# Feed-forward blocks taken in pairs with one accumulation per pair, and a norm without ordering edges, in a two-layer RWKV-7 / S5 trunk

## The chip, the cores and the metric

The kernel runs on one core of a Trainium2 chip. The metric is the device time of one execution in microseconds; a run's time is compared as the median of several. Engines are named as in the profile: PE (TensorE, matmul), PEld (TensorE's weight loads), DVE (VectorE), ACT (ScalarE), POOL (GpSimd), SP (SyncE, which issues most DMAs).

## What is computed

Two layers over 1024 frames of 1024 channels, in float32. Layer 0 mixes in time by an RWKV-7 recurrence, layer 1 by an S5 diagonal state-space layer with GELU and a gated output. After each mixer comes a feed-forward block, and every sub-layer ends in a norm:

```python
def sq_relu_mlp(x, w1, w2):
    return jnp.square(jax.nn.relu(x @ w1)) @ w2          # w1 1024x4096, w2 4096x1024

def reference(x, ...):
    h = x
    for i in range(2):
        mix = rwkv7_time_mix(h, ...) if i == 0 else s5_mix(h, ...)
        h = layer_norm(ALPHA * h + mix, ln_g[2 * i], ln_b[2 * i])
        h = layer_norm(ALPHA * h + sq_relu_mlp(h, mlp_w1[i], mlp_w2[i]), ln_g[2 * i + 1], ln_b[2 * i + 1])
    return h
```

## The kernel before

**Layout and precision.** Activations lie with channels on the 128 partitions and frames along the free dimension. The 1024 frames are two halves, A (`hA`, H = 0) and B (`hB`, H = 1), of 512 frames; a half is eight tiles of 128x512. A float32 product is made of three matmuls (`mm3`, line 258): each operand is split into a high part (a ScalarE cast, line 191) and a low part (a VectorE subtraction, line 192), and high x high, high x low and low x high are added up in one PSUM bank. Weights come by DMA as 128x512 pieces (`wraw`), are split into `whi` and `wlo` (three buffers each, `wraw` two), and each piece serves twelve matmuls. For the first three blocks of layer 1 the low parts of the weights are made beforehand (`presplit`) and loaded, so those blocks need only the cast (line 224).

**Feed-forward in blocks** (`blocks`, line 1110 on). The 4096 hidden channels are 16 blocks of 256. `up(b)` computes two 128x512 tiles of hidden channels, 24 matmuls into one bank each; ScalarE empties the bank with Relu (line 1126), squares (line 1127), and the result is split into `qbuf` (four slots, two for even and two for odd blocks). `down(b)` multiplies by the second weight matrix: four column groups `n2` of two tiles; each of the eight output tiles takes 6 matmuls in a bank of its own, and VectorE adds the bank to `h` (line 1158; line 1156 for the first block, which also scales by ALPHA). Banks come in rotation from `psd()`: three in layer 0 (`narrow`), seven in layer 1's feed-forward (`wide`).

`mlp` runs a half in layer 0 with the up phase one block ahead:

```python
up(0)
for b in range(nb):
    if b + 1 < nb: up(b + 1)
    down(b, b == 0)
    yield
```

**Order of the work.** A list scheduler orders each engine's instructions at compile time: lower priority numbers first, in a simulated time. `rank(base)` sets the number for what is traced inside it, and the feed-forward of layer 0 runs from 200000. So the rest of the recurrence, output projection, norms (99000) and S5 (99300, 99400) go ahead of it and its matmuls fill the gaps; the S5 tables (300000) come behind it. Work of another stage is also spread by hand: `first_steps` makes a generator's steps ready, and `weave` advances them behind each split (share `PACEU`) and each addition (share `PACED`); `behind` then adds an ordering edge, so that the woven VectorE instruction comes after the one that it is woven behind. `INS1`, `INS3` and `PREB` count the calls of `mlp` after which half B's output projection is traced, S5's result is loaded and the presplit starts.

**Layer 1's feed-forward.** Blocks 0 to 2 (`JB` = 3) of half A run alone (`ua`, `da`) while half B gets its norm (`second_half`, woven). Then `both` takes blocks 3 to 15 of the two halves together with sums and differences of operands (`tops`: T1 to T4, made of `hA` and `hB`; T1 goes into the buffer of `qbuf`, `t1b`). Then blocks 0 to 2 of half B run alone (`ub`, `db`), the last two of them by column halves of 256 frames with kept weights (`keep`, `kept`), so that `last_norm` of the first 256 frames can run beside the second.

Of the kernel before, what the change touches and what calls it, by code (L numbers as in the profile page):

```python
# [18 lines left out]
HT = 512  # L19
KT = 8  # L20
L = 64
KB2 = 2
INS1 = 12
INS2 = 13
VSH = (-1, 2, 2, 4, 64)
INS3 = 12
PACE = None
LN1R = -1
WO0R = 99000
# [3 lines left out]
TB = 2  # L33
LN2R = 99000
PAUSE = 8
PRE = 6
PACEU = (2.0, 7.0)
PACED = (0.5, 1.3)
PREB = 3
JB = 3  # L40
TABB = 6
LN8R = 400000
# [37 lines left out]
def trunk(ctx, tc, A):  # L80
# [102 lines left out]
    def unweave():  # L183
        while woven:
            steps, base = woven.pop(0)
            with rank(base):
                for _ in steps:
                    pass
# [15 lines left out]
    nw = [0]  # L204

    low = {}

    def wload(src, kt, n, key=None, halved=False):

        step = 512 // n  # L210
        out = []
        for k0 in range(0, kt, step):
            kept = low.get((key, k0)) if key else None
            raw = wp.tile([128, step, n], F32, tag="wraw", name="wraw", bufs=2)
            SP.dma_start(raw, src[:, k0 : k0 + step])
            hi = wp.tile([128, step, n], F32R, tag="whi", name="whi")
            lo = wp.tile([128, step, n], F32R, tag="wlo", name="wlo")
            nw[0] += 1
            if halved:
                S.mul(hi, raw, 0.5)  # L220
                weave(V.scalar_tensor_tensor(lo, raw, 0.5, hi.bitcast(F32), op0=ALU.mult, op1=ALU.subtract))
            elif kept is not None:
                SP.dma_start(lo.bitcast(F32).rearrange("p k n -> p (k n)"), kept)
                S.copy(hi, raw)
            else:
                split(raw, hi, lo, G if nw[0] % WLG[0] in WLG[1] and WLG[2] <= nw[0] < WLG[3] else V)
                if key and key[0] not in ("mw1", "mw2"):
                    low[key, k0] = dr.tile([128, 512], F32, name=f"low{len(low)}")
                    SP.dma_start(low[key, k0], lo.bitcast(F32).rearrange("p k n -> p (k n)"))
            out += [(hi[:, k], lo[:, k]) for k in range(step)]  # L230
        return out
# [26 lines left out]
    def mm3(p, whi, wlo, xh, xl, first, last):  # L258
        mmb(p, whi, xh, start=first, stop=False)
        mmb(p, whi, xl, start=False, stop=False)  # L260
        mmb(p, wlo, xh, start=False, stop=last)
# [18 lines left out]
    def dense(p, w, xs):  # L280
        n = len(xs)
        for k in range(n):
            mm3(p, w[k][0], w[k][1], xs[k][0], xs[k][1], k == 0, k == n - 1)
# [15 lines left out]
    def psd():  # L299
        pool, tag = banks[0][nb[0] % len(banks[0])]  # L300
        nb[0] += 1
        return pool.tile([128, HT], F32, tag=tag, name="d")
# [811 lines left out]
    def blocks(i, h, xo, qbuf):  # L1114

        nw = 512 // KB2
        qs = {}

        def up(b):
            qs[b] = []  # L1120
            pace_[0] = PACEU[i]
            for n in range(KB2):
                p = psd()
                dense(p, wload(A["mw1"][i, b * KB2 + n], KT, 128, ("mw1", i, b * KB2 + n)), xo)
                r = tp.tile([128, HT], F32, tag="ev", name="rl", bufs=EVB)
                S.activation(r, p, AF.Relu)  # L1126
                S.activation(r, r, AF.Square)
                qt = qbuf[:, n + KB2 * (b % 2)]
                split(r, qt[:, 0], qt[:, 1])
                qs[b].append((qt[:, 0], qt[:, 1]))  # L1130
            pace_[0] = 1.0

        def kept(src, part):
            raw = wp.tile([128, KB2, nw], F32, tag="wraw", name="wraw", bufs=2)
            SP.dma_start(raw, src)
            hi, lo = (jp.tile([128, HT], F32R, tag=t, name="k" + t, bufs=8).rearrange("p (k n) -> p k n", k=KB2)
                      for t in ("t1", "t2"))
            SP.dma_start(lo.bitcast(F32).rearrange("p k n -> p (k n)"), part)
            S.copy(hi, raw)
            return [(hi[:, k], lo[:, k]) for k in range(KB2)]  # L1140

        def down(b, first=False, cs=slice(0, HT), keep=None):
            for n2 in range(C // nw):
                if keep is None:
                    w = wload(A["mw2"][i, b, n2], KB2, nw, ("mw2", i, b, n2))
                else:
                    if (b, n2) not in keep:
                        keep[b, n2] = kept(A["mw2"][i, b, n2], low[("mw2", i, b, n2), 0])
                    w = keep[b, n2]
                for n in range(nw // 128):  # L1150
                    p = psd()[:, cs]
                    dense(p, [(x[:, n * 128 : (n + 1) * 128], y[:, n * 128 : (n + 1) * 128]) for x, y in w],
                          [(x[:, cs], y[:, cs]) for x, y in qs[b]])
                    z = h[n2 * (nw // 128) + n][:, cs]
                    if first:
                        weave(V.scalar_tensor_tensor(z, z, ALPHA, p, op0=ALU.mult, op1=ALU.add), PACED[i])
                    else:
                        weave(V.tensor_add(z, z, p), PACED[i])  # L1158

        return up, down  # L1160

    def mlp(i, h, xo, qbuf):

        nb = 32 // KB2
        up, down = blocks(i, h, xo, qbuf)
        up(0)
        for b in range(nb):
            if b + 1 < nb:
                up(b + 1)
            down(b, b == 0)  # L1170
            yield

    def both(i, hP, hQ, P, Q, tops, first):
# [400 lines left out]
    def first_steps(steps, base):  # L1574
        with rank(base):
            next(steps)
            woven.append([steps, tc.cur_priority])
# [66 lines left out]
    def second_half():  # L1644
        yield from norm_steps(hB, 2, 1, True, xoB)
        for k in range(4):
            a = t3[k]
            G.tensor_add(a, a, hB[k])
            d = [jp.tile([128, HT], F32R, tag="t2", name="t2", bufs=8) for _ in range(2)]
            split(a, *d)  # L1650
            yield 1
            tops[1].append(d)

    ua, da = blocks(1, hA, xo, qbuf)
    ua(0)
    first_steps(second_half(), 99000)
    for b in range(JB - 1):
        ua(b + 1)
        da(b, b == 0)
    unweave()  # L1660
    t1b = qtile()
    with rank(99100):
        for k in range(4):
# [5 lines left out]
        for k in range(4):  # L1669
            V.tensor_sub(t3[k], t3[k], hB[k + 4])  # L1670
            tops[3].append(operand(t3[k]))
    da(JB - 1, JB == 1)
    uj, dj = both(1, hB, hA, xoB, xo, tops, JB)
    uj(JB)
    for b in range(JB + 1, NB):
# [6 lines left out]
    with rank(99000):  # L1682
        layer_norm(hA, 3, 0, False)
    store(0, hA)
    for b in range(JB - TB):
        ub(b + 1)
        db(b)
    for b in range(JB - TB + 1, JB):
        ub(b)
    keep = {}  # L1690
    for c in range(2):
        for b in range(JB - TB, JB):
            db(b, False, slice(256 * c, 256 * c + 256), keep)
        if c == 0:
            with rank(LN8R):
                early = last_norm(hB, 3, 0)
                next(early)
# [74 lines left out]
```

## Time and profile before

| | |
|---|---|
| median of 3 runs | 2596.31 us (2596.01 to 2599.6) |
| the profiled execution | 2585.47 us, its span 2583.5 us |
| PE busy | 2466.0 us (95%), 16684 matmuls |
| DVE busy | 1794.0 us (69%) |
| ACT busy | 1210.5 us (47%) |
| POOL busy | 406.0 us (16%) |
| granted TensorE clock, mean | 0.975 |
| moved by DMA | 340.66 MB |

Shares are of the span. A matmul's recorded time overlaps its neighbours', so a busy PE is not a PE at its peak. Rows of the waits view read "engine line waited for: us in total, times, longest". Rows of the timeline give start, length, engine, line, operation, output<-inputs, shape, count, and in brackets the idle time before with what ended it.

### The profile page before, as it was taken

What the parts mean: (1) busy time and instruction counts of PE and PEld (TensorE: products, weight loads), DVE (VectorE), ACT (ScalarE), POOL (GpSimd) and SP (SyncE); (2) the same over time, 40 slices, a digit from 0 to 9 for tenths busy, and PEclk for the clock granted to TensorE, in tenths of its full rate; (3) what the DMA queues carried; (4) which work ended last, traced back from release to release, by engine and by line L of the source; (5) the groups of instructions that cost most, each with busy time, mean ns of one, the idle gap of its engine ahead of it and who ended that gap; (6) DMA issues with size and microseconds to landing.
All of it is one profiled execution on the core that took longest, in us unless ns stands there. A gap on an engine that the chain in (4) does not pass through costs nothing.

```text
span 2583.5 us, 43873 instructions
## 1 busy us (share of the span) xinstructions
PE 2466.0 (95%) x16684; PEld 2002.0 (77%) x16684; DVE 1794.0 (69%) x3443; ACT 1210.5 (47%) x2165; POOL 406.0 (16%) x336
## 2 busy tenths in 40 slices
PE   7989989989989999999999999999999999999997
PEld 5779767788767888777777878887887888888886
DVE  7477687577787776899886665676657555656555
ACT  7555575454454443345634444334565333343334
POOL 3110441331211102001000000100222111111111
PEclk9999989999899999999999999999999999999998
DMA  4765455664222324446565553244261111111233
GB/s 152 261 200 184 160 198 172 190 186 152 93 70 78 104 86 126 141 122 165 162 226 192 176 175 111 95 162 160 94 197 60 49 54 50 48 58 49 78 122 114
DMA packets 217682, 340.66 MB, mean 132 GB/s; under 512 B 21248, under 2 KB 81792, under 8 KB 217472
## 3 DMA queue, kind: packets, MB, share of 16 engines
q1 hardware_dynamic: 216320, 335.77, 40.9%
q8 instruction: 131, 2.15, 0.4%
q10 hardware_dynamic: 1152, 2.10, 0.2%
q14 instruction: 79, 0.65, 0.1%
HBM read 267.53 MB, written 70.25 MB: 131 GB/s over the span
## 4 chain that ended last, share of the span: by engine, by line
PE 69%; DVE 13%; DMA 9%; ACT 5%; issue 3%; SPq 1%; POOL 0%; ACTq 0%; DVEq 0%; POOLq 0%
PE d L256 51%; PE d L1195 10%; DVE wlo L192 2%; PE pA L672 1%; DMA wraw<-in_mw_dram 1%; ACT whi L191 1%; DMA yl<-s_y 1%; DVE hA L1158 1%; DMA pre<-in_mw_dram 1%; DMA ldsg<-s_sg 1%; DMA s_y<-yg 1%; PE pR L780 1%; DMA lda<-s_a 1%; DVE oAl L192 1%; PE pq L934 1%
## 5 line engine op out<-in xcount | busy, mean ns | idle before, releaser
L191 ACT CAST whi<-wraw 128x512 fp32r<-128x512 f32 x424 | 261.6, 619 | 487.1 <-PE d L256 249.8
L192 DVE TENSOR_TENSOR wlo<-wraw,whi 128x512 fp32r<-128x512 f32 x424 | 317.4, 750 | 201.1 <-ACT whi L191 197.2
L256 PE MATMUL d<-qbuf,whi 128*128 128x512 f32 x1152 | 365.2, 399 | 9.8 <-ACT rl L1126 4.7
L256 PE MATMUL d<-oAh,whi 128*128 128x512 f32 (+1 forms) x752 | 303.2, 409 | 13.1 <-ACT ev L493 5.5
L256 PE MATMUL d<-oAl,whi 128*128 128x512 f32 (+1 forms) x752 | 302.1, 403 | 7.7 <-DVE oAl L942 4.4
L256 PE MATMUL d<-oAh,wlo 128*128 128x512 f32 (+1 forms) x752 | 301.2, 404 | 3.5 <-DMA wlo<-low 1.9
L256 PEld LDWEIGHTS d<-qbuf,whi 128*128 128x128 f32 x1152 | 212.2, 189 | 63.1 <-DVE hA L1158 7.8
L256 PE MATMUL d<-qbuf,wlo 128*128 128x512 f32 x576 | 225.5, 394 | 0.0
L256 PE MATMUL d<-oBh,whi 128*128 128x512 f32 x496 | 195.9, 395 | 0.4 <-DVE hA L1158 0.4
L256 PE MATMUL d<-oBh,wlo 128*128 128x512 f32 x496 | 195.8, 395 | 0.0
L256 PE MATMUL d<-oBl,whi 128*128 128x512 f32 x496 | 193.7, 391 | 0.0
L256 PEld LDWEIGHTS d<-oAh,whi 128*128 128x128 f32 (+1 forms) x752 | 143.1, 192 | 48.0 <-ACT ev L493 7.8
L256 PEld LDWEIGHTS d<-oAl,whi 128*128 128x128 f32 (+1 forms) x752 | 144.4, 193 | 38.7 <-DVE oAl L942 4.8
L256 PEld LDWEIGHTS d<-oAh,wlo 128*128 128x128 f32 (+1 forms) x752 | 144.3, 193 | 36.2 <-DVE wlo L192 2.7
L256 PE MATMUL d<-ql,whi 128*128 128x512 f32 x416 | 163.1, 392 | 0.0
L256 PE MATMUL d<-qh,whi 128*128 128x512 f32 x416 | 162.0, 389 | 0.0
L256 PE MATMUL d<-qh,wlo 128*128 128x512 f32 x416 | 158.0, 394 | 0.0
L256 PEld LDWEIGHTS d<-qbuf,wlo 128*128 128x128 f32 x576 | 108.9, 189 | 24.4 <-issue 0.5
L1158 DVE TENSOR_TENSOR hA<-hA,d 128x512 f32<-128x512 f32 x136 | 92.0, 683 | 28.8 <-PE d L256 27.7
L1158 DVE TENSOR_TENSOR hB<-hB,d 128x512 f32<-128x512 f32 (+1 forms) x160 | 97.6, 631 | 20.1 <-PE d L256 18.9
L256 PEld LDWEIGHTS d<-oBh,wlo 128*128 128x128 f32 x496 | 93.2, 188 | 21.9 <-issue 0.8
L256 PEld LDWEIGHTS d<-oBh,whi 128*128 128x128 f32 x496 | 93.3, 188 | 21.5 <-issue 2.0
(495 smaller groups left out, 5268.6 us busy)
## 6 DMA issues: line engine op xcount, KB each, us to landing
wraw<-in_mw_dram SPq DMA_DIRECT2D x356, 256.0 KB, 2.7
wlo<-low SPq DMA_DIRECT2D x92, 256.0 KB, 2.9
wraw<-in_glu_dram SPq DMA_DIRECT2D x64, 256.0 KB, 2.7
low<-wlo SPq DMA_DIRECT2D x52, 256.0 KB, 2.6
raw<-in_mw_dram SPq DMA_DIRECT2D x52, 256.0 KB, 2.7
wraw<-in_wk_dram SPq DMA_DIRECT2D x32, 256.0 KB, 3.2
wraw<-in_wr_dram SPq DMA_DIRECT2D x32, 256.0 KB, 3.7
wraw<-in_wv_dram SPq DMA_DIRECT2D x32, 256.0 KB, 4.2
```

Source lines behind the costliest of these rows:

```text
L191: S.copy(hi, src)
L192: op = (e or V).tensor_sub(lo, src, hi.bitcast(F32))
L256: bulk.append((PE.matmul(p, w, x, **kw).ins, x.shape[-1]))
L672: prods.append(PE.matmul(pp[h][:, cc, i], D.KB[j][hs, u].rearrange("p j l -> p (j l)"), D.AR[j][hs, u].rearrange("p j l -> p (j l)"), star ...
L780: hop.append(PE.matmul(pR[hs, i], at[:, h, c, i, 0], vsa[:, cl, h, i], start=True, stop=True))
L934: PE.matmul(pq[:, j : j + 1], q[:, j * 128 : (j + 1) * 128], ones_c[:, 0:1], start=k + j == 0, stop=k == KT - 1, skip_group_check=True)
L1158: weave(V.tensor_add(z, z, p), PACED[i])
L1195: PE.matmul(p, w[:, k], x, start=not add and k + j == 0, stop=k == 3 and j == 2, skip_group_check=True)
```

## The change

`down` takes a tuple of blocks and adds up all their products for an output tile in one bank, so that VectorE adds to `h` once per tuple. `mlp` and layer 1's blocks alone call it with pairs. The up phases of both blocks of a pair stand ahead of its down phase. The products of a column group are ordered by block; in the first group (`n2 == 0`) of a pair the second block's two operands are taken one after the other over both output tiles. In layer 1 half B's norm and T2 are traced at once under rank 99000, without weaving and so without ordering edges, behind the first up phase; blocks 0 and 1 of half A form a pair and block 2 stands alone. At the end, the last two blocks form a pair within each column half. `INS1` and `INS3` go from 12 calls to 6, `PREB` from 3 to 1, and the shares `PACEU` and `PACED` of layer 1 change, where nothing is woven in `blocks` any more.

```diff
-INS1 = 12
+INS1 = 6
-INS3 = 12
+INS3 = 6
-PACEU = (2.0, 7.0)
-PACED = (0.5, 1.3)
-PREB = 3
+PACEU = (2.0, 6.0)
+PACED = (0.5, 2.0)
+PREB = 1
...
-        def down(b, first=False, cs=slice(0, HT), keep=None):
+        def down(bs, first=False, cs=slice(0, HT), keep=None):
             for n2 in range(C // nw):
...
+                ws = []
+                for b in bs:
+                    if keep is None:
+                        ws.append(wload(A["mw2"][i, b, n2], KB2, nw, ("mw2", i, b, n2)))
...
+                nn = nw // 128
+                ps = [psd()[:, cs] for _ in range(nn)]
+                parts = [(w[k], qs[b][k]) for w, b in zip(ws, bs) for k in range(KB2)]
...
+                last = len(parts) - 1
+                groups = [range(KB2 * m, KB2 * m + KB2) for m in range(len(bs))]
+                if n2 == 0 and len(bs) > 1:
+                    groups[-1:] = [(j,) for j in groups[-1]]
+                turns_ = [(n, js) for js in groups for n in range(nn)]
+                for n, js in turns_:
+                    products(n, js)
+                    if last not in js:
+                        continue
+                    z, p = h[n2 * nn + n][:, cs], ps[n]
...
     def mlp(i, h, xo, qbuf):
...
-        up(0)
-        for b in range(nb):
-            if b + 1 < nb:
-                up(b + 1)
-            down(b, b == 0)
+        for b in range(0, 32 // KB2, 2):
+            up(b)
+            up(b + 1)
+            down((b, b + 1), b == 0)
             yield
...
     ua(0)
-    first_steps(second_half(), 99000)
-    for b in range(JB - 1):
-        ua(b + 1)
-        da(b, b == 0)
-    unweave()
+    with rank(99000):
+        run(second_half())
+    ua(1)
+    da((0, 1), True)
+    ua(2)
...
-    da(JB - 1, JB == 1)
+    da((2,))
...
-    for b in range(JB - TB):
-        ub(b + 1)
-        db(b)
-    for b in range(JB - TB + 1, JB):
-        ub(b)
+    ub(1)
+    db((0,))
+    ub(2)
     keep = {}
     for c in range(2):
-        for b in range(JB - TB, JB):
-            db(b, False, slice(256 * c, 256 * c + 256), keep)
+        db(tuple(range(JB - TB, JB)), False, slice(256 * c, 256 * c + 256), keep)
```

More of the change, by code (lines that the diff above doesn't have):

```diff
@@ L1140, in kept, with products @@
             return [(hi[:, k], lo[:, k]) for k in range(KB2)]
-        def down(b, first=False, cs=slice(0, HT), keep=None):
+        def down(bs, first=False, cs=slice(0, HT), keep=None):
             for n2 in range(C // nw):
[L1144 to L1154, printed above, removed]
+                ws = []
+                for b in bs:
+                    if keep is None:
+                        ws.append(wload(A["mw2"][i, b, n2], KB2, nw, ("mw2", i, b, n2)))
+                    else:
+                        if (b, n2) not in keep:
+                            keep[b, n2] = kept(A["mw2"][i, b, n2], low[("mw2", i, b, n2), 0])
+                        ws.append(keep[b, n2])
+                nn = nw // 128
+                ps = [psd()[:, cs] for _ in range(nn)]
+                parts = [(w[k], qs[b][k]) for w, b in zip(ws, bs) for k in range(KB2)]
+                def products(n, js):
+                    for j in js:
+                        (x, y), (qh, ql) = parts[j]
+                        sl = slice(n * 128, (n + 1) * 128)
+                        mm3(ps[n], x[:, sl], y[:, sl], qh[:, cs], ql[:, cs], j == 0, j == len(parts) - 1)
+                last = len(parts) - 1
[8 more added lines that the diff above has]
+                    z, p = h[n2 * nn + n][:, cs], ps[n]
                     if first:
@@ L1162, in mlp @@
     def mlp(i, h, xo, qbuf):
-        nb = 32 // KB2
         up, down = blocks(i, h, xo, qbuf)
-        up(0)
-        for b in range(nb):
-            if b + 1 < nb:
-                up(b + 1)
-            down(b, b == 0)
+        for b in range(0, 32 // KB2, 2):
+            up(b)
+            up(b + 1)
+            down((b, b + 1), b == 0)
             yield
```

## The prediction

> **What bounds the kernel now.** I read the page's busy times first, then the stages as stretches, then TensorE's waits stage by stage, then the timeline at the places where the edit acts.
>
> ```profile
> PE 2466.0 (95%) x16684; PEld 2002.0 (77%) x16684; DVE 1794.0 (69%) x3443; ACT 1210.5 (47%) x2165; POOL 406.0 (16%) x336
> L1158 DVE TENSOR_TENSOR hA<-hA,d 128x512 f32<-128x512 f32 x136 | 92.0, 683 | 28.8 <-PE d L256 27.7
> L1158 DVE TENSOR_TENSOR hB<-hB,d 128x512 f32<-128x512 f32 (+1 forms) x160 | 97.6, 631 | 20.1 <-PE d L256 18.9
> ```
>
> TensorE is busy 95% of the span; the edit changes neither the number of matmuls (16684) nor their shapes. It can only fill or open gaps in TensorE's stream. The stages (columns: length, then busy time of PE, PEld, DVE, ACT, POOL, then the granted clock and DMA):
>
> ```profile
> 740.00:1020.00 280.00, 275.03 (x2170) 220.09 (x2169) 210.29 (x459) 123.90 (x226) 38.57 (x30) 0.99 0.31 93
> 1020.00:1280.00 260.00, 252.50 (x1288) 196.02 (x1287) 233.75 (x452) 125.01 (x228) 23.02 (x18) 0.99 0.52 149
> 1280.00:1570.00 290.00, 281.27 (x2011) 227.89 (x2009) 194.75 (x359) 129.23 (x227) 0.00 (x0) 1.00 0.56 188
> ```
>
> From 740 to 1640 runs layer 0's feed-forward for both halves, mixed with the end of the recurrence, the S5 tables and S5. TensorE idles there 5.0, 7.5 and 8.7 us in the three rows: this is all that the pairs can win. What ended TensorE's idle times from 740 to 1570, and then from 1885 to the end (us in total, times, longest):
>
> ```profile
> PE d L256 <- ACT rl L1126: 4.7, 6, 1.6
> PE d L256 <- DVE hA L1158: 3.9, 5, 1.8
> ...
> PE d L256 <- DVE hA L1156: 0.7, 1, 0.7
> ```
>
> ```profile
> PE d L1195 <- DVE wlo L192: 4.1, 1, 4.1
> PE d L256 <- ACT rl L1126: 2.2, 1, 2.2
> ...
> PE d L256 <- DVE hA L1158: 0.6, 1, 0.6
> ```
>
> The waits on L1156 and L1158 are for a PSUM bank that the addition into h has not yet emptied; those on L1126 for a bank that the Relu has not yet emptied. The rest of the idle time in the first stretch belongs to the recurrence, the S5 tables and S5, out of the edit's reach.
>
> **The change part by part.**
>
> *One addition per pair.* Full-width additions fall from 136 to 64 on hA and from 128 to 64 on hB, and the 32 half-width ones of the last stage to 16. At 0.683 us each that is 136 x 0.683 = 93 us less VectorE work (16 half ones at some 0.4 us make it about 100), so VectorE goes from 1794 to about 1695. By itself this shortens nothing, VectorE not being the bound. What counts is the bank waits. Matmuls come every 0.2287 us:
>
> ```profile
> 1559.65 93.09 PE d L256 x407
> ```
>
> Before, a bank of the down phase took 6 matmuls, 1.37 us, and with three banks in rotation was wanted back 2 x 1.37 = 2.7 us after it was full. In the pair it takes 12 matmuls; of each column group's two banks one is wanted back after 2.7 us as before (2.1 in the first group) and the other after 5.5. So it is less the room for one addition that grows than the pile behind it that shrinks: one addition in 2.7 us, beside one wlo subtraction, instead of two. I let 4.2 of the 3.9 + 0.7 + 0.6 = 5.2 us go (ends: 2.5 and 5.2).
>
> *Relu bank waits.* The last Relu of an up phase had 2.7 us before its bank was wanted (two short banks, then its turn). In the pair its bank comes up in the second column group, 24 matmuls or 5.5 us later. The 4.7 us of the first fence of waits go (ends: 3.5 and 4.7). But what made that Relu late stays, and is felt by what follows.
>
> *The operand of the second block: the new wait.* Before, block b+1's up phase stood ahead of block b's down phase, 48 matmuls (11 us) before its operand was read. Now the pair's down phase follows at once. In the first column group the second block's last operand is read after 12 products of the first block and 6 of the second block's other operand: 18 matmuls, 4.1 us after the up phase ends, and its low part one matmul later, 4.3 us. A clean case shows how long the operand takes:
>
> ```profile
> 1600.67 0.39 PE L256 MATMUL d<-oBh,wlo 128*128 128x512 f32 x1
> ...
> 1601.39 0.59 ACT L1126 ACTIVATE rl<-d 128x512 f32<-128x512 f32 x1
> 1602.02 0.63 ACT L1127 ACTIVATE rl<-rl 128x512 f32<-128x512 f32 x1
> 1602.68 0.62 ACT L191 CAST qbuf<-rl 128x512 fp32r<-128x512 f32 x1
> 1603.34 0.69 DVE L192 TENSOR_TENSOR qbuf<-rl,qbuf 128x512 fp32r<-128x512 f32 x1 [0.16 <-ACT qbuf L191]
> ```
>
> The last product's slot ends at 1600.67 + 0.23 = 1600.90; the low part is there at 1604.03, 3.1 us later: 1.2 us to spare. A late case:
>
> ```profile
> 1487.60 0.39 PE L256 MATMUL d<-oBh,wlo 128*128 128x512 f32 x1
> 1489.08 0.62 ACT L239 CAST prehi<-pre 128x512 fp32r<-128x512 f32 x1 [0.92 <-DMA pre<-in_mw_dram]
> 1491.23 0.62 ACT L191 CAST whi<-wraw 128x512 fp32r<-128x512 f32 x1 [1.53 <-DMA wraw<-in_mw_dram]
> 1491.75 0.59 ACT L1126 ACTIVATE rl<-d 128x512 f32<-128x512 f32 x1
> 1492.39 0.73 PE L256 MATMUL d<-qbuf,whi 128*128 128x512 f32 x2 [1.64 <-ACT rl L1126]
> 1493.69 0.69 DVE L192 TENSOR_TENSOR qbuf<-rl,qbuf 128x512 fp32r<-128x512 f32 x1 [0.52 <-ACT qbuf L191]
> ```
>
> ScalarE works in order and stands behind two casts that wait for transfers; the Relu starts at 1491.75, the low part is ready at 1494.38, 6.55 us after 1487.83: 2.2 us over the 4.34. In this way I compared the second operand of all 16 odd blocks of layer 0, whose Relus start between 757.76 and 1623.33; they are 16 of these:
>
> ```profile
> L1126 ACT ACTIVATE rl<-d x76: 574/591/600, 738.7 to 2538.9; 128x512 f32<-128x512 f32 x76
> ```
>
> Eight are over: 3.9, 3.3, 3.0, 0.7 on half A; 2.2, 1.4, 0.2, 2.2 on half B; 17 us in all. The lower end is 0. The upper end assumes that TensorE has nothing else, but the first, second and sixth fall where recurrence, output projection or S5 products go between (each lengthens the 4.3 us), the next column group's first bank offers six products more (1.4 us), and the three of half A were late behind additions and table work on VectorE, of which half the additions go. Nearest row: the Relu waits, 4.7 us in 32 up phases, felt at half as many places with 0.4 us less room and one more engine in the chain. I take 5.5 us. Queued behind a waiting product is all of TensorE's stream; weights are read in the same order, twelve products a tile, so their buffers see no change.
>
> *The last stage's norm without ordering edges.* Before, VectorE did little while the norm of half B was paced; then the rest piled up at the end:
>
> ```profile
> 1878.99 0.69 DVE L985 TENSOR_TENSOR sa<-sa,sb 128x512 f32<-128x512 f32 x1
> ...
> 1896.85 2.47 DVE L993 TENSOR_TENSOR hB<-hB,pm 128x512 f32<-128x512 f32 x4
> ...
> 1932.79 1.74 POOL L192 TENSOR_TENSOR oBl<-hB,oBh 128x512 fp32r<-128x512 f32 x1
> 1933.30 1.78 DVE L192 TENSOR_TENSOR oBl<-hB,oBh 128x512 fp32r<-128x512 f32 x1
> 1949.53 0.69 DVE L192 TENSOR_TENSOR wlo<-raw,whi 128x512 fp32r<-128x512 f32 x1
> ```
>
> The sum was ready at 1879.7, the subtractions began 17 us later, and `both`'s first low part was made only at 1949.53, which is the 4.1 us wait on L1195. Unpaced, the norm starts about 14 us earlier and its pile is gone by 1945: I take 3.6 us of gain (ends: a loss of 2, if the burst delays the casts of weights, and a gain of 4.1). For the burst falling on the pair's operands I add 0.5 (ends 0 and 3): the same norm work stood beside the second and third block before, and the second fence of waits shows no wait for weights on line 256.
>
> A rule of the Trainium skill speaks against the burst: "SBUF — State Buffer", section Who interferes with whom, says that a VectorE instruction with two SBUF inputs contends with GpSimd reads. The trace agrees: beside GpSimd's 1.74 us the subtraction at 1933.30 took 1.78 instead of 0.69. Were the operand of the pair hit once, it would cost 1.1 us more, and the sum below would be -5.9 instead of -7.0.
>
> *The last pair by column halves.* Before, the second block's second operand was late here too:
>
> ```profile
> 2533.02 4.27 PE L256 MATMUL d<-qbuf,kt 128*128 128x256 f32 x36
> 2538.87 0.57 ACT L1126 ACTIVATE rl<-d 128x512 f32<-128x512 f32 x1
> 2539.50 11.47 PE L256 MATMUL d<-qbuf,kt 128*128 128x256 f32 x84 [2.21 <-ACT rl L1126]
> 2543.66 0.69 DVE L192 TENSOR_TENSOR qbuf<-rl,qbuf 128x512 fp32r<-128x512 f32 x1 [1.79 <-ACT qbuf L191]
> 2563.04 0.43 DVE L1036 TENSOR_TENSOR sab<-hB 128x256 f32<-128x256 f32 x1
> ```
>
> TensorE filled the time with the first block's products of both halves (36, then more). Accumulating in one bank, each bank can take 9 of its 12 products before the late operand; seven banks give 63 x 0.119 = 7.5 us, to about 2540.5, and the high part comes at 2543.7: a wait of 3.3 where there was 2.2, so +1.1. In return the first half's norm begins sooner and the second half's sums (2563.04) need not stand behind it after the last addition: about -1.6. Together -0.5 (ends -2.5 and +4). The bank waits ended by L1126 in this stage are in this term.
>
> Gathered weave counts and moved constants (12 blocks become 6 pairs, the presplit starts after the fourth block either way) cost nothing: the cover is that norm and presplit have 4 and 8 blocks for their steps, as before; without it, a few us at the start of half B.
>
> Sum: -4.2 - 4.7 + 5.5 - 3.6 + 0.5 - 0.5 = -7.0 us. The profiled execution took 2585.47 us (span 2583.5), 10.8 us less than the median 2596.31 of the runs; I apply the difference to the median: 2589.3 us, -0.3%.
>
> **The rivals.** (1) No change: pair ends cost 11 us instead of 5.5, as if two thirds of the 17 were felt: sum -1.5, 2594.8. For it: ScalarE's waits for transfers stay as they are. Against: TensorE's other work at these places. (2) Slower: the pair ends decide. From 5.5 + 7.0 = 12.5 us, 0.78 us a pair, the gain is gone; if also blocks that were in time become late, at 1.3 us on each of 16 pairs, it is 21 us, and the sum +8.5: 2604.8. For it: eight of sixteen already over, and VectorE 90% busy from 1020 to 1280. Against: a clean block needs 3.1 of the 4.3 us. (3) The edges were not what delayed L1195: its 4.1 us stay or turn into waits in the first pair; sum -3.4 or worse, 2592.9, inside no change. (4) More is won: relieved VectorE also brings the table products in time and the operands with them, 5 us more: 2584.3.
>
> **How the numbers follow.** Forecast as summed or better with (4): 0.53, of which (4) 0.13. Rival (1) 0.19, (3) 0.11: together 0.30 for no change. Rival (2): 0.17. A difference of 0.2% (5.2 us) is about what a measurement of this kernel can tell. The range is 2581 to 2601: below it lies the tail of (4), above it most of (2). The likeliest case's own range is 2584 to 2591.
>
> **What would show it.** Right: L1158 with x64 and x80, VectorE near 1695 us; no TensorE wait on L1158, none on L1126 before 1640; new waits of TensorE on `qbuf` (L192 or L191) of 4 to 8 us at pair ends, most at 1020 to 1280 and 1395 to 1570; no 4.1 us wait on L1195. Wrong: qbuf waits over 13 us, a wait for `whi` at 1890 to 1930, or an end that moves by more than 2 us after the last product.

## The result and the profile after

The changed kernel took 2582.88 us (median of 9 runs, 2572.66 to 2590.97) beside 2594.06 us of the kernel before, measured with it (9 runs, 2585.37 to 2599.6): a ratio of 0.9952, 95% interval 0.993 to 0.9973. That is faster, by 0.5% where 0.3% was forecast, and inside the range. The profiled execution has a span of 2581.1 us. Of all runs below, one each of e2 (3016 us), e10 (3971 us) and the kernel before (11688 us) were far slower than the rest; the medians include them, the ratios do not. How much of this is the change itself is a question of its own: the same kernel measured a second time came out at 0.9991 (below).

The page of the changed kernel, and its groups of additions (line 1158 has become 1175 and 1156 has become 1173; the S5 lines have moved by 15):

```profile
PE 2469.3 (96%) x16684; PEld 2004.9 (78%) x16684; DVE 1709.7 (66%) x3291; ACT 1211.1 (47%) x2165; POOL 407.2 (16%) x336
L1175 DVE TENSOR_TENSOR hB<-hB,d 128x512 f32<-128x512 f32 (+1 forms) x80 | 49.1, 629 | 23.2 <-PE d L256 22.7
L1175 DVE TENSOR_TENSOR hA<-hA,d 128x512 f32<-128x512 f32 x64 | 42.5, 681 | 23.4 <-PE d L256 23.3
```

The additions are x64 and x80 as forecast, 98 us less of recorded time, but VectorE's busy time fell by 84 us only (1794.0 to 1709.7, forecast 1695). An addition behind another instruction overlaps it by some 0.08 us: five in a row take 3.08 us (from 1949.46 on), 0.60 each for all but the last, where one alone is recorded with 0.68.

What ended TensorE's idle times from 742 to 1652, the stretch that was 740 to 1640 before:

```profile
PE d L256 <- DVE wlo L192: 4.0, 2, 3.6
PE pyt L1563 <- DVE yg L1565: 3.8, 3, 1.9
PE d L256 <- DVE hB L1175: 2.5, 1, 2.5
PE d L256 <- ACT whi L191: 2.5, 5, 0.8
PE py L1545 <- DVE oAl L1512: 2.0, 1, 2.0
PE d L256 <- DVE hA L1175: 1.3, 1, 1.3
```

No line has `rl` any more, and none has `qbuf` as the releaser: neither the old Relu waits nor the new operand waits that were forecast are there. In their place stand waits for weights (`wlo`, `whi`) and for S5 (`yg`, `oAl`): 6.5 us for weights and 5.8 us on `yg` and `oAl`; before, they came to 0.3 and 2.1 us. With the smaller rows the sum is the same: idle times over 0.15 us between the first Relu and the gated output add up to 20.7 us before and 20.0 after. From 1884 to the end the rows that bear on the change are:

```profile
PE d L256 <- ACT kt L1139: 1.3, 1, 1.3
...
PE d L256 <- ACT qbuf L191: 1.1, 1, 1.1
...
PE d L256 <- DVE qbuf L192: 0.5, 1, 0.5
```

The 4.1 us on L1195 are gone, and at block 2, which stands alone, TensorE waits 1.6 us for its operand. The 1.3 us on L1139 are for the high part of a weight of the last pair.

To see where time went in runs that differ by several us in places no edit touches, I cut each profile at fixed events: the first Relu of layer 0 (S0 ends), the first product of the gated output (L0 ends), the first product of layer 1's feed-forward, the sixth product of `both`, its last one, and the first and last half-width product. Lengths in us; e1 to e12 are the experiments below, and the stretch from the last product of `both` to the first half-width one is 88.5 in all of them.

| | S0 | L0 | gated output | layer 1 alone | both | half-width | end | span |
|---|---|---|---|---|---|---|---|---|
| before | 738.7 | 905.97 | 231.91 | 74.31 | 493.67 | 27.62 | 22.86 | 2583.5 |
| after | 742.7 | 908.88 | 232.70 | 71.10 | 492.00 | 26.26 | 18.98 | 2581.1 |
| e1 pairs of layer 0 only | 741.7 | 908.21 | 232.35 | 74.31 | 493.94 | 25.07 | 23.30 | 2587.4 |
| e2 norm only | 743.9 | 912.17 | 230.13 | 71.35 | 492.00 | 25.70 | 23.30 | 2587.1 |
| e3 last pair only | 752.1 | 904.72 | 230.29 | 73.95 | 493.93 | 26.55 | 20.61 | 2590.6 |
| e4 all, again | 746.9 | 912.28 | 232.18 | 70.77 | 492.00 | 26.41 | 18.98 | 2588.0 |
| e5 second block first | 738.8 | 918.09 | 230.95 | 72.92 | 492.20 | 26.28 | 20.58 | 2588.3 |
| e6 half the additions | 746.9 | 901.42 | 228.44 | 74.13 | 494.54 | 25.39 | 22.82 | 2582.1 |
| e7 one step a split | 751.5 | 891.06 | 230.91 | 70.89 | 492.00 | 26.18 | 18.98 | 2570.0 |
| e8 single blocks in layer 0 | 739.5 | 903.48 | 231.36 | 70.90 | 492.00 | 26.54 | 18.98 | 2571.3 |
| e9 single, one step a split | 740.2 | 912.11 | 235.28 | 72.61 | 492.00 | 29.45 | 20.28 | 2590.4 |
| e10 1.5 steps a split | 747.5 | 894.19 | 229.17 | 72.70 | 492.00 | 26.28 | 20.62 | 2571.0 |
| e11 one step, presplit too | 746.2 | 897.05 | 231.13 | 71.37 | 492.00 | 28.06 | 20.67 | 2574.9 |
| e12 presplit later | 748.3 | 909.16 | 232.53 | 72.66 | 492.00 | 26.43 | 20.67 | 2590.3 |

S0, which is the same code everywhere, scatters by 13 us. L0 scatters too: it is 903.5 to 912.2 us in the four kernels that have the same single blocks there (before, e2, e3, e8). Most of this shows in the traces as idle times and as stretches at half clock. By the clock records, half clock costs 3.4 us of L0 in before, e3 and e8 and 8.5 in e2, 5.1 to 8.5 in after, e1, e4 and e12, and none in e7; what is left of L0 without it and without the idle times lies between 879 and 886 us in all fourteen. The span alone therefore says little about one part of the edit, and the stretch that the part acts in says more.

### The profile page after: what moved, and what is told of

The parts are those of the page before. It is cut to its first block, busy times and chain, and to the rows that moved or that the text cites. A ratio compares the mean times of both kernels' runs of the same rounds, so it can differ in the third digit from the quotient of the medians.

```text
span 2581.1 us, 43650 instructions
## 1 busy us (share of the span) xinstructions
PE 2469.3 (96%) x16684; PEld 2004.9 (78%) x16684; DVE 1709.7 (66%) x3291; ACT 1211.1 (47%) x2165; POOL 407.2 (16%) x336
## 5 line engine op out<-in xcount | busy, mean ns | idle before, releaser
L191 ACT CAST whi<-wraw 128x512 fp32r<-128x512 f32 x424 | 261.8, 619 | 471.2 <-PE d L256 240.1
L256 PE MATMUL d<-qbuf,whi 128*128 128x512 f32 x1152 | 360.0, 397 | 6.3 <-DVE hB L1175 2.5
L256 PEld LDWEIGHTS d<-oBl,whi 128*128 128x128 f32 x496 | 93.3, 188 | 20.9 <-issue 0.8
L224 ACT CAST whi<-wraw 128x512 fp32r<-128x512 f32 x92 | 56.8, 618 | 105.4 <-PE d L256 75.4
```

Of the source, the lines that this page charges most:

```text
L191: S.copy(hi, src)
L256: bulk.append((PE.matmul(p, w, x, **kw).ins, x.shape[-1]))
```

## The experiments

**The change in its parts.** Each of the first three takes one part of the diff: e1 the pairs of `mlp` with their constants, e2 the norm of half B at once under rank 99000 with blocks one by one, e3 the tuple of two blocks in the loop over column halves. e4 is the changed kernel again. The lines of e2 and of e3:

```
-    first_steps(second_half(), 99000)
+    with rank(99000):
+        run(second_half())
     for b in range(JB - 1):
         ua(b + 1)
         da(b, b == 0)
-    unweave()
...
-        for b in range(JB - TB, JB):
-            db(b, False, slice(256 * c, 256 * c + 256), keep)
+        db(tuple(range(JB - TB, JB)), False, slice(256 * c, 256 * c + 256), keep)
```

> Pairs in layer 0 alone; layer 1's norm, its three blocks and the last two blocks as before. By the steps of the prediction (bank waits -3.7, Relu waits -4.7, second operand +5.5) 2.9 us less than before. Rival, read from the trace of the changed kernel (from layer 0's first Relu to the first product of the gated output 906.0 us before, 908.9 after): nothing, 0 to +3 us. Second rival: the 87 us less of VectorE work are the whole gain, -8 us or more. In the trace: no TensorE wait on L1126 and none on qbuf; waits for wlo and whi of 4 to 7 us in their place.

> The kernel before with half B's last norm and T2 traced at once, without weaving and edges; blocks one by one as before. Theory: the edges delayed the first low part of the sums' stage, so the 4.1 us wait on L1195 goes and the stretch from layer 1's first up phase to that stage is 3 to 4 us shorter; time -3 to -5 us. Rival: the wait has another cause and stays: 0. Second rival: the burst delays weights or operands: 0 to +3, with waits for whi or qbuf.

> Only the last two blocks by column halves add up in one bank; all else as before. By the prediction's step -0.5 us (a longer wait for the late operand, +1.1, and sums that need not stand behind the first half's norm, -1.6). Rival, read from the trace of the changed kernel (last stage from the first half-width product to the end 50.5 us before, 45.2 after): -4 to -5 us, most of it after the last product.

> The changed kernel itself once more beside its parts. If the parts add up, its difference to before is the sum of the three others within 4 us. By the prediction -7 us, by the first measurement -11. In the trace the part up to layer 0's first Relu, which the edit doesn't touch, differs by up to 4 us between runs (738.7 before, 742.7 after in the first two), and the later stages agree with the first profile of the changed kernel within 2 us each.

Ratios to the kernel before: e1 0.9988 (0.997 to 1.0006), e2 0.9964 (0.9948 to 0.998), e3 0.9999 (0.9981 to 1.0018), e4 0.9991 (0.9975 to 1.0007). e4 is the code that had 0.9952 (0.993 to 0.9973) before. The two intervals do not meet, so a ratio of this kernel carries more scatter than its interval says, and the 0.4% of e2 are no proof by themselves. Nor do the parts add up to e4 as whole times: 3.1, 9.3 and 0.3 us, against 2.3 us. The stages are:

- L0 with single blocks (before, e2, e3, and e8 below): 905.97, 912.17, 904.72, 903.48, mean 906.6. With pairs (after, e1, e4, e12): 908.88, 908.21, 912.28, 909.16, mean 909.6. The pairs of layer 0 bring no gain there; if anything they cost 3 us, which is less than either group scatters. e1 has 6.5 us of waits for weights and no Relu wait, as the changed kernel has.
- The norm: layer 1 alone and `both` together take 567.98 and 568.25 us without it (before, e1) and 563.10, 563.35, 562.77 with it (after, e2, e4), some 5 us less; over the whole table 562.8 to 565.1 with it and 567.9 to 568.7 without, in the means 4.5 us apart. In all kernels with the norm `both` is 492.0 to 492.2, in all without it 493.7 to 494.5. The ordering edges and the pacing went together in e2, so which of the two had delayed the norm is not told apart.
- The last pair: half-width and end together take 50.5, 48.4 and 49.0 us without it (before, e1, e2), and 45.2, 47.2 and 45.4 with it (after, e3, e4). Of the later kernels with the pair (all but e6), e9 (49.7) and e11 (48.7) lie among those without.

**What single blocks in layer 0 make of the rest.**

```
-        for b in range(0, 32 // KB2, 2):
-            up(b)
-            up(b + 1)
-            down((b, b + 1), b == 0)
+        nb = 32 // KB2
+        up(0)
+        for b in range(nb):
+            if b + 1 < nb:
+                up(b + 1)
+            down((b,), b == 0)
-INS1 = 6
+INS1 = 12
-INS3 = 6
+INS3 = 12
-PREB = 1
+PREB = 3
```

> The changed kernel, but layer 0 takes its blocks one by one as before; the norm without ordering edges with the pair in layer 1 and the last pair by column halves stay. Theory A (the pairs of layer 0 bring nothing; the gain is the norm's and the last stage's): the stretch from the first Relu to the gated output's first product at 904 to 912 us as before, and the whole within 0.15% of the changed kernel, about 0.4% below the kernel before. Rival (the prediction's -3.4 us for layer 0's pairs is there and drowns in the scatter): 3 to 5 us slower than the changed kernel, a ratio to the kernel before of about 0.997.

Measured: 2579.49 us, ratio 0.9957 (0.9941 to 0.9973), L0 903.48. The old waits are back, and the time is that of the changed kernel's first measurement:

```profile
PE d L256 <- DVE hA L1175: 4.1, 5, 2.1
PE d L256 <- ACT rl L1126: 3.7, 4, 1.4
```

So the gain of the change does not need layer 0's pairs, as far as two ratios of this scatter can tell; L0 itself says the same.

**The operand of the second block.** The pair's order in `mlp`:

```
-            down((b, b + 1), b == 0)
+            down((b + 1, b), b == 0)
```

> The changed kernel, but in layer 0 the pair's down phase takes the second block's products first. Its last operand is then wanted 3 matmuls (0.7 us) after the up phase instead of 18 to 19 (4.3 us), while a clean operand takes 3.1 us. Theory (the changed kernel escapes the wait on the operand because the first block's products cover it): without the cover TensorE waits for qbuf at most of the 16 pair ends, some 2.4 us each where nothing else is at hand, so 20 to 39 us of new waits, and the stretch from the first Relu to the gated output's first product grows from about 909 to 930 to 950 us. Rival (the list scheduler brings other products forward in any case, and the order inside the pair hardly matters): under 8 us of qbuf waits and a stretch under 920 us.

Measured: ratio 0.9991 (0.9973 to 1.001), L0 918.09, some 8 us over the pairs' mean. Waits of TensorE in L0:

```profile
PE d L256 <- ACT rl L1126: 5.6, 4, 3.3
PE d L256 <- ACT qbuf L191: 3.5, 7, 1.9
```

The waits on `qbuf` are 3.5 us where the theory had 20 to 39, and L0 is below 920: the rival holds in both its numbers. Beside it stand 5.6 us of Relu waits, and half clock costs 11.9 us of L0 here. The order of issue of the changed kernel shows how the operand is covered. Here is the pair end behind 1444, from the last of the 18 products on, and in the last line VectorE's low part of the late operand:

```profile
1448.13 0.39 PE L256 MATMUL d<-qbuf,wlo 128*128 128x512 f32 x1
1448.88 0.71 PE L1563 MATMUL pyt<-ident,y 64*128 64x64 f32 x8 [0.37 <-DVE yg L1565]
1449.53 0.73 PE L256 MATMUL d<-qbuf,whi 128*128 128x512 f32 x2
1450.10 0.40 PE L256 MATMUL d<-qbuf,wlo 128*128 128x512 f32 x1
1450.33 0.62 PE L256 MATMUL d<-qbuf,whi 128*128 128x512 f32 x2
1450.79 0.39 PE L256 MATMUL d<-qbuf,wlo 128*128 128x512 f32 x1
1451.02 1.07 PE L256 MATMUL d<-qbuf,whi 128*128 128x512 f32 x4
...
1450.70 0.69 DVE L192 TENSOR_TENSOR qbuf<-rl,qbuf 128x512 fp32r<-128x512 f32 x1 [1.28 <-ACT qbuf L191]
```

Behind the 18 products and S5's turn the compile-time scheduler has put six more, in the order of one bank's six (twice two with `whi` and one with `wlo`), before four with `whi` in a row open the late operand. The view leaves out the numbers of banks; that these six are the next column group's first bank is read from their order. So 24 matmuls and S5's turn stand ahead instead of 18. The low part came 7.1 us after the up phase here, and TensorE did not wait for it.

**Fewer additions without pairs.** The kernel before, with line 1158 changed; the additions of layer 0's odd blocks are left out.

```
+                        if i == 0 and b % 2:
+                            continue
-                        weave(V.tensor_add(z, z, p), PACED[i])
+                        weave(V.tensor_add(z, z, p), 2 * PACED[i] if i == 0 else PACED[i])
```

> The kernel before, with the additions of layer 0's odd blocks left out (128 of 256; their products are made and thrown away), and the remaining ones advance the woven work by twice the share; the order of the blocks is as before. It shows what fewer additions are worth without pairs. Theory A (the prediction's term: additions are what delays the banks): TensorE's waits for a bank on the addition fall from 4.8 us to under 1, those on the Relu from 4.7 to some 3, and the stretch from the first Relu to the gated output's first product falls by 4 to 6 us, to about 902. Theory B (VectorE is a queue in order, and table, norm and split work that stands in front of an addition decides): the waits move to other producers on VectorE, TensorE's idle time in the stretch stays within 3 us of 21, and the stretch at 904 to 910.

Measured: ratio 0.9954 (0.9935 to 0.9974), L0 901.42, idle there 16.0 us. The rows (1160 is the addition, 1156 that of the first block):

```profile
PE d L256 <- ACT rl L1126: 4.0, 4, 1.4
...
PE d L256 <- DVE hA L1160: 2.2, 4, 0.8
...
PE d L256 <- DVE hB L1156: 1.2, 1, 1.2
PE d L256 <- DVE hB L1160: 0.9, 1, 0.9
```

Half the additions are gone and the waits on the rest are still 4.3 us of 4.8. Theory A has the length of the stretch right and its reason wrong: an addition is late for something other than the other additions. Theory B misses both of its numbers too (idle within 3 us of 21, stretch 904 to 910). What stands ahead on VectorE in place of the additions was not tried apart, and the additions that are left carry twice the woven steps here.

**The share of woven steps.** In the changed kernel the longest wait of L0 is the one on `wlo` that ends at 1126.79. TensorE's row, and VectorE's rows in front of it:

```profile
1126.79 0.50 PE L256 MATMUL d<-oAh,wlo 128*128 128x512 f32 x1 [3.56 <-DVE wlo L192]
```

```profile
1118.99 4.27 DVE L993 TENSOR_TENSOR hB<-hB,pm 128x512 f32<-128x512 f32 x7
1123.17 0.69 DVE L1430 TENSOR_TENSOR tw<-pw,bc 128x512 f32<-128x512 f32 x1
...
1126.05 1.29 DVE L192 TENSOR_TENSOR wlo<-wraw,whi 128x512 fp32r<-128x512 f32 x2
```

Seven subtractions of half B's norm in a row: the norm is woven behind splits, two steps each, and two up phases in a row have twice the splits before the next addition. The five rows from 1123.17 to 1126.05 are work on the S5 tables, which stands there in e7 and e10 too. Three kernels change only this share in half A's feed-forward (e7: 1, e10: 1.5), or take 1 with single blocks (e9, on top of e8); e11 is e7 with 1 for the presplit in half B too.

```
-            pace_[0] = PACEU[i]
+            pace_[0] = 1.0 if i == 0 and h is hA else PACEU[i]
```

> The changed kernel, but during half A's feed-forward of layer 0 each split advances the woven norm of half B by one step instead of two. Theory A (two up phases in a row gather the woven steps in front of a low part of a weight): the single wait of 3.6 to 4.1 us on wlo near 1126 and the half clock behind it go; TensorE's waits for weights in layer 0 fall from some 6.5 to 3 us, the stretch from the first Relu to the gated output's first product from about 910 to about 904, and the whole by 4 to 6 us. Theory B (VectorE has no room there, and the steps only collide elsewhere): the wait moves to another low part, an addition or an S5 operation, idle time in the stretch stays at 19 to 21 us, and the whole is within 0.1%.

> Layer 0's blocks one by one as before, the rest as in the changed kernel, and half B's woven norm in half A's feed-forward advances one step a split instead of two: the fourth corner beside single blocks at two steps, pairs at two and pairs at one. Theory A (the share was too high for two up phases in a row; with single blocks the steps are spread already): little changes, the stretch from the first Relu to the gated output's first product at 901 to 909 us (903.5 at two steps), the whole within 0.15% of single blocks at two steps (about 0.9957 of the kernel before). Then the pairs are worth some 10 us at the lower share. Theory B (the lower share is worth the same whatever the order of the blocks): the stretch at 888 to 896 us, the whole at 0.990 to 0.992, and the pairs of layer 0 bring nothing at either share.

> The changed kernel with 1.5 woven steps a split in half A's feed-forward of layer 0, between the 2 of the changed kernel (stretch 908.2 to 912.3 us, whole about 0.9955 of the kernel before) and the 1 of the gentle one (891.1 us, 0.991). Theory A (the pile of woven steps in front of a weight's low part is the cause, and it grows with the share): a stretch of 893 to 904 us, a whole of 0.991 to 0.994, and a wait on wlo near 1126 of 1 to 3 us. Rival (any other schedule would have done, the lower share found a lucky one): the wait near 1126 is gone or as long as before without the time following it, and waits at other places than at either share.

> As the gentle kernel (one woven step a split in half A's feed-forward), and the presplit of weights in half B's feed-forward too at one step a split instead of two. Theory A (there VectorE is free enough; the gentle kernel shows no wait on an addition or a weight behind 1300): within 0.15% of the gentle kernel, a stretch of 889 to 895 us. Rival (the presplit's casts and subtractions, which wait for their transfers, still hold up what is behind them in half B): 2 to 5 us faster, a stretch under 889.

Measured, beside the two shares of 2 from above:

| L0 blocks, share | median us | ratio to before | L0 us | idle in L0 |
|---|---|---|---|---|
| single, 2 (e8) | 2579.49 | 0.9957 (0.9941 to 0.9973) | 903.48 | 20.0 |
| single, 1 (e9) | 2589.4 | 0.9995 (0.998 to 1.001) | 912.11 | 26.8 |
| pairs, 2 (after; e4) | 2582.88; 2584.55 | 0.9952; 0.9991 | 908.88; 912.28 | 20.0; 20.5 |
| pairs, 1.5 (e10) | 2572.17 | 0.9921 (0.99 to 0.9942) | 894.19 | 8.5 |
| pairs, 1 (e7) | 2567.46 | 0.991 (0.9885 to 0.9936) | 891.06 | 11.1 |
| pairs, 1, presplit 1 (e11) | 2574.53 | 0.9936 (0.9915 to 0.9956) | 897.05 | 14.1 |

The subtractions in a row and the wait behind them at 1.5 and at 1 step (each kernel's VectorE, then its TensorE):

```profile
1122.94 2.47 DVE L993 TENSOR_TENSOR hB<-hB,pm 128x512 f32<-128x512 f32 x4
...
1128.95 0.80 PE L256 MATMUL d<-oAh,wlo 128*128 128x512 f32 x1 [2.17 <-DVE wlo L192]
```

```profile
1127.43 1.27 DVE L993 TENSOR_TENSOR hB<-hB,pm 128x512 f32<-128x512 f32 x2
...
1132.24 0.50 PE L256 MATMUL d<-oAh,wlo 128*128 128x512 f32 x1 [1.01 <-DVE wlo L192]
```

Seven, four, two; 3.56, 2.17, 1.01 us: this wait grows with the pile, and theory A of e7 and e10 holds for it. The pile does not explain all that the lower share brings. L0 shrinks by 18.5 us at one step and by 15.4 at 1.5 (from the mean of 909.6). By the idle times and the clock records, 8.5 of the 18.5 are idle time, 6 half clock and 4 neither; of the 15.4, 11 are idle time, 1 half clock and 3 neither. With the half clock behind it (below) the wait near 1126 accounts for some 4 and 1.5 us; most of the other idle time lay in half B, on `yg`, `oAl`, `hB` and `whi`, in waits that e7 and e10 hardly have. In e7 S5 is through at 1388 (its last `pyt`) and all but one of the presplit's 24 subtractions stand behind it; in the changed kernel S5 ends at 1449 and the presplit stands in it from 1337. But e10 has the presplit and S5 at the same places as the changed kernel and still lacks those waits, but for `oAl`. With single blocks the lower share brings no gain, so theory B of e9 falls. Theory A misses its numbers too: L0 is 912.11 us and not 901 to 909, and the ratio 0.9995 and not about 0.9957. But e2 has as long an L0 with two steps, and the changed kernel's two ratios differ as much, so a loss by the lower share is not shown. At one step the stretch is 21 us shorter with pairs than with single blocks, in one profile each. e11's rival falls: the presplit is no better spread at one step, and a new Relu wait of 3.6 us stands at 1580.

**The presplit later.** In the changed kernel:

```
-PREB = 1
+PREB = 2
```

> The changed kernel (two woven steps a split), with the presplit of layer 1's weights started after the third pair of half B instead of the second. In the changed kernel the presplit's subtractions run from 1337 on among S5's own operations, in the single-block kernels from about 1394, when S5 is nearly done. Theory A (the presplit among S5's chain makes the waits of half B: 3.8 us for yg, 2.0 for oAl, 2.5 for an addition on hB, with some 1.4 us of half clock): these go, the stretch from the first Relu to the gated output's first product falls from about 910 to 899 to 903 us, the whole to 0.992 to 0.993 of the kernel before; the wait of 3.6 to 4.1 us on wlo near 1126 stays. Rival (the waits of half B hang on how the scheduler happens to place things; at 1.5 steps a split the presplit stands at the same place without them): the stretch changes by less than 4 us, or waits of the same sum come at other places of half B.

Measured: ratio 0.9988 (0.9975 to 1.0001), L0 909.16. The rival holds: the waits on `yg` and `hB` shrink (6.3 to 3.4 us), those on `whi` and S5's transfer grow (2.8 to 6.2). But S5 lasts until 1463 here, and six of the presplit's subtractions still stand before its last `pyt`, where ten did: e12 moved the presplit without taking it out of S5. That its place alone does not make the waits is seen in e10, not here. Why half B loses its waits at the lower shares stays open; that some other order would have done so too is not excluded by three kernels.

e7 is the best version: 0.991 of the kernel before, in six runs. Its interval lies below those of e2, e3, e8 and e9, which keep layer 0's blocks one by one, and below e4's; it meets that of the changed kernel's first measurement (0.993) at its upper end, and those of e10 and e11 overlap with it. It was measured beside e8, not beside the changed kernel itself, which enters by its ratios alone.

## Why the prediction was right or wrong, step by step

The direction came out and the time fell into the range, but of the six terms two are well sized, and the largest cost is not there. That the total is near is in part luck: in layer 0 the operand's +5.5 us did not come, and in its place came late weights and late S5 work that had no price.

- **Bank waits on additions, -4.2: mis-sized.** In L0 they fell from 4.6 (mean of the four kernels with single blocks) to 3.7 us (after, e1, e4; 0.9 in e12), and in layer 1 by 0.6, so -1.5. The pile behind an addition was not other additions alone (e6). What stands ahead now is seen at 1456: TensorE waits 2.52 us for a bank while the addition stands on VectorE behind an S5 step and a presplit subtraction, whose cast waited 2.23 us for its transfer.

```profile
1453.42 0.62 ACT L239 CAST prehi<-pre 128x512 fp32r<-128x512 f32 x1 [2.23 <-DMA pre<-in_mw_dram]
1454.07 0.69 DVE L240 TENSOR_TENSOR pre<-pre,prehi 128x512 fp32r<-128x512 f32 x1 [1.48 <-ACT prehi L239]
1454.68 1.12 DVE L1565 SCALAR_TENSOR_TENSOR yg<-hA,pv,pyt 128x512 f32<-128x512 f32 x1
...
1455.72 1.27 DVE L1175 TENSOR_TENSOR hB<-hB,d 128x512 f32<-128x512 f32 x2
...
1456.45 1.22 PE L256 MATMUL d<-qbuf,whi 128*128 128x512 f32 x2 [2.52 <-DVE hB L1175]
```

- **Relu waits, -4.7: right.** 4.7, 5.6, 5.5 and 3.7 us with single blocks (before, e2, e3, e8); none in after, e1 and e4, 0.2 in e12.
- **The second block's operand, +5.5: wrong.** There is no such wait in L0. The failing step is "In the first column group the second block's last operand is read after 12 products of the first block and 6 of the second block's other operand: 18 matmuls". The prediction took the products in the order in which the program lists them; the scheduler moves them. It had named the cover (six products of the next column group, other stages' work) and still charged 5.5 us. The lateness itself was as forecast in kind: five of sixteen low parts came after the 4.34 us, 10.4 us in all, where eight with 17 us were counted before. But in these five 74, 50, 24, 34 and 22 matmuls started before the low part was there, and TensorE never waited for it.
- **"Gathered weave counts … cost nothing" and "weights are read in the same order … so their buffers see no change": wrong**, and the largest new wait stands here. The order is the same, but the work around it is not: two up phases in a row gather the woven steps (seven subtractions before 1126.05). TensorE waited for weights for 6.5 to 7.7 us in after, e1, e4 and e12, where it was 0.3 to 0.8 with single blocks; 3.2 to 4.1 us of it is the one wait behind the pile. The prediction gave "a few us at the start of half B" in case the steps did not fit; this wait came in half A. With it, waits on S5's `yg` and `oAl` grew from 1.7 to 4.9 us (means of four), and these have no cause that was shown. The edit was priced by what it does to TensorE's order, and not by what its order of tracing does to VectorE's.
- **The norm, -3.6 and +0.5: right in mechanism, a little small.** The sum's last step and the subtractions behind it, after:

```profile
1886.77 0.69 DVE L985 TENSOR_TENSOR sa<-sa,sb 128x512 f32<-128x512 f32 x1
...
1892.89 4.87 DVE L993 TENSOR_TENSOR hB<-hB,pm 128x512 f32<-128x512 f32 x8
```

  They begin 5.4 us after the sum is ready instead of 17, all eight in a row. The 4.1 us are gone and the pair's operands saw no burst; but the work of rank 99100 now falls on block 2, whose operand waits:

```profile
1942.35 1.26 PE L256 MATMUL d<-qbuf,whi 128*128 128x512 f32 x4 [1.08 <-ACT qbuf L191]
1944.14 0.50 PE L256 MATMUL d<-qbuf,whi 128*128 128x512 f32 x1 [0.53 <-DVE qbuf L192]
```

  That +1.6 is paid by a term that nobody put in: `both` begins at full clock, and takes 1.7 us less. The first view is before, around the 4.1 us wait and behind it, the second after, at the same stage (the column before the last two is the granted clock):

```profile
1945.80:1950.30 4.50, 0.44 (x3) 0.03 (x1) 4.50 (x9) 2.88 (x6) 0.00 (x0) 0.99 0.00 0
1950.30:1954.00 3.70, 3.70 (x9) 2.94 (x10) 3.70 (x6) 0.00 (x0) 1.28 (x1) 0.55 0.22 71
```

```profile
1950.00:1954.00 4.00, 4.00 (x19) 3.32 (x18) 4.00 (x8) 1.56 (x3) 0.00 (x0) 1.00 0.39 133
```

  The price of 1.1 us that was weighed here for an operand of the pair did not fall due: no low part of the pair's operands took over 0.8 us, and the slowest low part of a Relu's result, 1.42 us, stands at 2516.
- **The last pair, -0.5: right in sign, small.** The wait of 3.3 us for the late operand did not come: TensorE waited 1.33 us, where 2.21 had been, and what ended it was a weight's cast (`kt`), which ScalarE made ahead of the operand's. The second half's sums follow their last addition at once (2562.57, then 2562.91) and no longer stand behind the first half's norm. The tail is 3.9 us shorter; "an end that moves by more than 2 us" was named as a sign of error, and it is one of size. But 1.7 us of it are chance (see the last section): the four kernels without the pair have half clock at these rows, of the ten with it after, e4, e7 and e8 do not. The rows of the changed kernel and of e12, whose last stage is the same code, are

```profile
2564.06 1.13 PE L1045 MATMUL pm<-sab,ones_c 128*128 128x256 f32 x4
2565.02 1.03 PE L1045 MATMUL pm<-hB,ones_c 128*128 128x256 f32 x4
```

```profile
2571.47 2.04 PE L1045 MATMUL pm<-sab,ones_c 128*128 128x256 f32 x4
2573.30 1.84 PE L1045 MATMUL pm<-hB,ones_c 128*128 128x256 f32 x4
```

- **Sum.** By stages: L0 +3.0 (means of four and four), the norm about -4.5, the last stage -2.2 (mean of the ten kernels with the pair, 46.8, less that of the four without, 49.0): about -4, or 0.15%. The forecast was -7.0; the two measurements, 0.9952 and 0.9991, are -12 and -2. By stages rival (1), no change, is as near as the forecast, though for another reason than pair ends; rivals (2) and (3) are out, and (4) is not what happened.

## What to carry to other kernels

When phases that issue helper work are put next to each other, look at the queue of the engine that does the helper work: steps paced per instruction pile up where the instructions do, and a share tuned for the old order has to be set again (here 2 to 1 with pairs, worth more than the whole edit; with single blocks it brought nothing). A wait read off the program's order of products may be covered by a scheduler that reorders them; count what is issued ahead of the late operand before pricing it. And where an untouched stage scatters by more than the effect, compare the stage that the edit acts in, over several kernels that share it.

## What the runs showed of the hardware

**Half clock after short waits.** Behind the 3.56 us wait of the changed kernel the matmuls from 1128.28 to 1131.27 come every 0.43 us instead of 0.229:

```profile
1122.84:1127.00 4.16, 0.60 (x3) 0.21 (x2) 4.16 (x8) 3.33 (x7) 2.38 (x1) 1.00 0.00 0
1127.00:1131.00 4.00, 4.00 (x13) 3.17 (x13) 4.00 (x6) 1.88 (x4) 2.09 (x1) 0.66 0.36 131
```

That is 1.6 us more for a wait of 3.6. Shorter waits do it too, not always: the 2.17 us of e10 cost 1.6 us behind them, the 2.52 us at 1456 cost 1.4, and the same 1.25 us wait in the last stage, with eight one-column matmuls ahead of it, leaves the eight sums at full clock in four kernels with one code (after, e4, e7, e8) and at half clock, in whole or in part, in six (e3, e5, e9 to e12). The Trainium skill, "TensorE: Matmul & The Clock Gate", section "Part 1: The HAM clock gate (the "warmup" mystery)", describes a clock halved after an idle window of about 3.4 us that runs freely. The free-running window fits the chance seen here; that a whole idle window is needed does not, since 2.17 us, and 1.25 us behind thin work, were enough here.

The clock records say more. In each of the fourteen traces every half-clock stretch begins on a grid of 3.413 us, to within 1 ns; where the grid lies differs from trace to trace, and this is the chance. I counted TensorE's idle time in each cell of that grid at full clock, from 800 us to 50 us before the end, over all traces. Of 27 cells with more than 2.0 us, all were followed by half clock; of 33 with 1.5 to 2.0 us, 15 were; of 284 with some, but less, none. A wait that is split between two cells can go free where the same wait inside one costs up to 1.7 us more.

**An untouched stage that scatters.** S0 runs from 738.7 to 752.1 us by kernel. The granted clock goes with it; between 200 and 400 us it is 0.94 before and 0.89 in e7, and fewer matmuls are done in the same time:

```profile
200.00:400.00 200.00, 181.78 (x1876) 147.68 (x1873) 157.64 (x370) 123.70 (x234) 61.04 (x56) 0.94 0.56 181
```

```profile
200.00:400.00 200.00, 179.59 (x1812) 147.24 (x1810) 149.40 (x348) 119.40 (x226) 62.05 (x57) 0.89 0.53 171
```

Half clock costs 47.8 us of S0 in the kernel before and 66.6 in e7, and 64.9 in e3, whose S0 is the longest. What sets the clock there was not tried.
